# Squares of eight tiles summed on the vector engine and counted once, or counted tile by tile on the tensor engine behind twelve spare transposes

## The chip, the cores and the metric

One core of a Trainium2 chip runs the whole kernel. The metric is device microseconds (us) of one execution. The kernel before took a median of 2697.3 us over three runs (2695.89 to 2697.41).

## What is computed

Two layers of a transformer-like network run over 512 latent tokens and 256 context tokens, with 1024 features each. Only the very first step matters here: the RMS norm of the latents ahead of the first feed-forward block, and the modulation (shift and scale, a product of two conditioning vectors with a weight matrix) that is applied to it.

```
def rms_norm(x, g):
    xf = x.astype(jnp.float32)
    y = xf * lax.rsqrt(jnp.mean(xf * xf, axis=-1, keepdims=True) + EPS)
    return (y * g.astype(jnp.float32)).astype(x.dtype)

def modulate(h, shift, scale):
    return h * (1 + scale) + shift

def half_ffn(h, g, shift, scale, gate, wg, wu, wd):
    return h + 0.5 * gate * swiglu(modulate(rms_norm(h, g), shift, scale), wg, wu, wd)
```

The latents are kept transposed: features on the 128 partitions, tokens along the free dimension. So the 1024 features are eight tiles `xT[0..7]` of 128 x 512 (the context's 256 columns lie beside them), and the mean of the squares of one token is a sum over the partitions of eight tiles.

## The kernel before

The engines are in-order queues: TensorE (PE, with its weight loads PEld), VectorE (DVE), ScalarE (ACT), GpSimd (POOL) and SyncE (SP, which issues almost all transfers). At the kernel's head the instructions stand on PE, DVE and ACT exactly in the order in which the code is written (`chain("te", "ve", "se")` up to the matching `unchain`); every one of them is recorded by one helper, so that nearly all of the profile's rows name its line, L67. Buffers come from rings: `temp()` gives one of five tiles `t`, `slot()` one of 34 tiles `s`, `po()` one of four single PSUM banks, `ps()` one of two double ones. Who takes a buffer waits until its last user is done.

The head goes as follows.

1. The conditioning vectors `sT` land, ACT takes their SiLU, and PE spreads them over all partitions by 16 transposes into two PSUM tiles (`sb_ps`, copied to `sb` much later).
2. The eight tiles `xT[k]` land one after the other. ACT squares each (`stl.square`). The first square goes to a slot `s`, the others to temps `t`; DVE adds squares 1 to 6 to the first (`stl.accumulate`), so that one tile holds the sum of seven.
3. `stl.sums(stl.sq)`: PE clears a bank with a matmul on zeros (`zero`), then counts two tiles into it (`count`): the sum of seven, and the eighth square. To count a tile is four matmuls, one for each 128 tokens, with the squares as weights and a 128 x 2 tile of ones as the moving operand. In float32 each of them is two instructions on PE, each with its weight load, so eight of each kind for a tile.
4. `stl.mean()` and `rsqrt` are nine short DVE instructions on a 128 x 4 tile. Meanwhile PE does five of the eight matmuls of the first modulation group, `wm0_mm(0, 0, 5)` (ten instructions, `ps<-s,sT`). Then `stl.spread(rl)`: four transposes spread the root over the partitions, ACT copies them to `Rs`, PE does the other three matmuls, `wm0_mm(0, 5, KD)`, and ACT copies their result (`sm<-ps`, `wm0_copy(0)`).
5. A loop over eight groups `g` follows: PE computes shift and scale of feature tile `g`, DVE and ACT split modulation weights and scale `xT[g]`, PE begins the first feed-forward products. From about 60 us on the feed-forward block proper runs.

Of the kernel before, what the change touches and what calls it, by code (L numbers as in the profile page):

```python
# [11 lines left out]
AF = mybir.ActivationFunctionType  # L12
# [3 lines left out]
P = 128  # L16
D = 1024
KD = D // P
# [14 lines left out]
LAT = slice(0, SEQ)  # L33
# [15 lines left out]
def tile_net(ctx: ExitStack, tc: tile.TileContext, a, out):  # L49
# [34 lines left out]
    te, ve, se, pe = Engine(nc.tensor, "te"), Engine(nc.vector, "ve"), Engine(nc.scalar, "se"), nc.gpsimd  # L84
# [7 lines left out]
    def nm(s):  # L92
        uid[0] += 1
        return f"{s}{uid[0]}"
# [4 lines left out]
    def temp(dt=F32, w=T):  # L99
        return pool.tile([P, w], dt, name=nm("t"), tag="t", bufs=NTMP)  # L100
# [4 lines left out]
    def ps():  # L105
        return psum.tile([P, 1024], F32, name=nm("ps"), tag="ps", bufs=2)

    def po():
        return psum.tile([P, 512], F32, name=nm("po"), tag="po", bufs=4)

    def f32(t):
        return t.bitcast(F32)
# [7 lines left out]
    ident = const.tile([P, P], F32, name="ident")  # L120
# [15 lines left out]
    xT = [const.tile([P, T], F32, name=f"xT{k}") for k in range(KD)]  # L136
# [105 lines left out]
    def tv(t, s):  # L242

        v = t[:, 0:T].rearrange("p (a b) -> p a b", b=HALF)
        if s == LAT:
            return v[:, :, 0:SEQ // 2]
        if s == CTXS:
            return v[:, :, SEQ // 2:HALF]
        return t[:, 0:SEQ // 2] if s.start == 0 else t[:, HALF:HALF + SEQ // 2]

    def cv(t, s, at=0):

        v = t[:, at:at + s.stop - s.start]
        return v.rearrange("p (a b) -> p a b", a=2) if s in (LAT, CTXS) else v
# [1750 lines left out]
    stl, stc = Stats(LAT, D), Stats(CTXS, D, ps)  # L2005
# [13 lines left out]
    def wm0_high(g):  # L2019
        if g in NATIVE:  # L2020
            return
        parts[g] = [(slot(F32R), slot(F32R)) for _ in range(3)]
        for i, t in enumerate(raws[g]):
            w = 256 * min(3, KD - 3 * i)
            se.copy(parts[g][i][0][:, :w], t[:, :w])
# [45 lines left out]
    for i in range(2):  # L2071
        sb.append(const.tile([P, D], F32, name=f"sb{i}"))
        sb_ps.append(ps())
        for k in range(KD):
            te.transpose(out=sb_ps[i][:, k * P:(k + 1) * P], in_=sT[:, k, i:i + 1].to_broadcast([P, P]), identity=ident)
    for k in range(KD):
        nc.sync.dma_start(out=tv(xT[k], LAT), in_=a["xT"][k, :, LAT].rearrange("p (a b) -> p a b", a=2))
        if k == 0:
            ve.tensor_copy(s4[:, :, 0:2], sT)
            ve.tensor_sub(s4[:, :, 2:4], sT, f32(s4)[:, :, 0:2])  # L2080
            ve.tensor_copy(sel[:, 0:2], ident[0:4, 0:2])
            ve.tensor_add(sel, sel, ident[0:4, 2:4])
        stl.square(tv(xT[k], LAT))
        if k < KD - 1:
            stl.accumulate()
    for i in range(2):
        se.copy(sb[i], sb_ps[i])
    gn.append(cload("gn0", a["gn"][0], [P, 3, KD]))
# [5 lines left out]
    m01 = [const.tile([P, KD, 2], F32, name=f"m01_{j}") for j in range(2)]  # L2094
    for j in range(2):
        mod[(0, j)] = [m01[j][:, :, i] for i in range(2)]
    stl.sums(stl.sq)
    wm0_high(0)
    wm0_low(0, 0)
    stl.mean()  # L2100
# [173 lines left out]
```

## Time and profile before

| | |
|---|---|
| median of three runs | 2697.3 us |
| the profiled execution's own time | 2700.62 us |
| its span, first to last instruction | 2698.8 us |
| PE busy | 2645.2 us, 98% of the span |
| DVE busy | 2047.8 us, 76% |
| ACT busy | 1140.2 us, 42% |
| PE clock granted, mean of the span | 0.996 |

A row of the timeline gives the start (us from the span's start), the time from the first start to the last end of the merged instructions, the engine, the line, the operation, what it writes and reads, the number of merged instructions and, in brackets, how long the engine had been idle before and what ended that. A row of the table by stretches gives, for each stretch, its length, the busy time and number of instructions of PE, PEld, DVE, ACT and POOL, the share of full speed at which the PE clock was granted, the busy share of the transfer engines and the rate in GB/s. The clock is 1.00 where the profile has no record of a cut, which includes the time ahead of its first record.

### The profile page before, as it was taken

Reading aid. Unit: us, or ns where it says so; the run is one execution under the profiler, and the core shown is the slowest. Engines: PE = TensorE matmul, PEld = TensorE weight load, DVE = VectorE, ACT = ScalarE, POOL = GpSimd, SP = SyncE. Lnnn points to the kernel's source line nnn. Section 1 sums busy time; section 2 is a strip of 40 time slices with the busy share of each in tenths; the row PEclk is TensorE's granted clock in tenths of the full one; section 3 lists DMA queues with packets and bytes.
Section 4 is the critical chain, followed back from the end, with each engine's and each line's share of the span. In section 5 each row is a group of like instructions: output and inputs, shape, how many; then the busy total and the mean of one; then the engine's idle time right before and its main releaser. Section 6 shows DMA issues by size and latency. Waiting matters only on the chain. (4 is left out here: it accounts for less than half of the span.)

```text
span 2698.8 us, 40531 instructions
## 1 busy us (share of the span) xinstructions
PE 2645.2 (98%) x16076; PEld 2512.7 (93%) x16076; DVE 2047.8 (76%) x3483; ACT 1140.2 (42%) x1977; POOL 147.5 (5%) x224
## 2 busy tenths in 40 slices
PE   8999999999989999999999999999999999999999
PEld 5999999999888889999999999999998888889988
DVE  6957777777689987777777777777766798776655
ACT  5323333441488633333334433333343488444433
POOL 0000000001230100000000000000000221011110
PEclk9999999999999999999999999999999999999999
DMA  7312333233100321233333223333224101245543
GB/s 254 125 47 94 110 109 110 94 101 136 33 1 9 112 101 56 102 108 110 103 109 105 68 83 104 110 106 105 97 83 162 49 9 40 95 132 169 160 126 118
DMA packets 102606, 266.07 MB, mean 99 GB/s; under 512 B 11920, under 2 KB 40336, under 8 KB 102416
## 3 DMA queue, kind: packets, MB, share of 16 engines
q1 hardware_dynamic: 95792, 249.32, 27.5%
q0 software_dynamic: 6624, 14.16, 2.6%
q8 instruction: 126, 2.06, 0.3%
q14 instruction: 64, 0.52, 0.1%
HBM read 256.63 MB, written 2.10 MB: 96 GB/s over the span
## 5 line engine op out<-in xcount | busy, mean ns | idle before, releaser
L67 PE MATMUL ps<-s,wh 128*128 128x384 f32 (+2 forms) x4224 | 968.4, 338 | 6.2 <-DVE xT L67 2.0
L67 PE MATMUL po<-s,wh 128*128 128x384 f32 (+2 forms) x3216 | 777.7, 327 | 1.1 <-ACT t L67 0.5
L67 PEld LDWEIGHTS ps<-s,wh 128*128 128x128 f32 x4224 | 730.2, 188 | 49.1 <-issue 5.1
L67 PE MATMUL ps<-s,wl 128*128 128x384 f32 (+2 forms) x2112 | 602.3, 337 | 1.3 <-DVE wl L67 1.2
L67 PEld LDWEIGHTS po<-s,wh 128*128 128x128 f32 x3216 | 563.4, 189 | 13.3 <-ACT s L67 0.8
L67 PE MATMUL po<-s,wl 128*128 128x384 f32 (+2 forms) x1608 | 525.6, 327 | 0.0
L67 PEld LDWEIGHTS ps<-s,wl 128*128 128x128 f32 x2112 | 381.2, 188 | 20.1 <-DVE wl L67 3.5
L67 PEld LDWEIGHTS po<-s,wl 128*128 128x128 f32 x1608 | 303.4, 189 | 5.9 <-DVE wl L67 0.2
L67 DVE SCALAR_TENSOR_TENSOR junk<-mr,sb 128x1024 fp8e4<-128x1024 f32 x224 | 273.0, 1219 | 15.0 <-DMA mr<-in_wm_dram 14.2
L67 DVE SCALAR_TENSOR_TENSOR xT<-ps,mod,xT 128x256 f32<-128x256 f32 (+1 forms) x360 | 198.1, 593 | 103.7 <-PE ps L67 101.8
L67 DVE TENSOR_TENSOR wl<-wr,wh 128x1024 fp32r<-128x1024 f32 (+3 forms) x158 | 188.9, 1198 | 110.0 <-ACT wh L67 109.6
L67 ACT CAST wh<-wr 128x1024 fp32r<-128x1024 f32 (+3 forms) x158 | 160.3, 1018 | 153.4 <-PE ps L67 85.9
L67 ACT COPY t<-po 128x384 f32<-128x384 f32 (+2 forms) x218 | 98.4, 451 | 264.1 <-PE po L67 263.5
L67 PE MATMUL po<-s,s 128*128 128x256 f32 (+3 forms) x1216 | 191.7, 309 | 5.5 <-DVE pl L67 2.1
L67 PEld LDWEIGHTS po<-s,s 128*128 128x128 f32 x1216 | 173.8, 191 | 12.6 <-DVE pl L67 2.4
L67 ACT ACTIVATE t<-t 128x384 f32<-128x384 f32 (+1 forms) x144 | 72.0, 500 | 260.6 <-DVE t L67 260.6
L67 DVE TENSOR_TENSOR t<-po,t 128x384 f32<-128x384 f32 (+2 forms) x226 | 117.2, 523 | 35.3 <-ACT t L67 24.9
L67 ACT CAST wh<-ws 128x1024 fp32r<-128x1024 f32 x72 | 75.7, 1052 | 155.1 <-PE ps L67 99.4
L67 ACT CAST s<-t 128x768 fp32r<-128x768 f32 (+3 forms) x144 | 93.0, 650 | 113.4 <-DVE t L67 109.2
L67 DVE TENSOR_TENSOR s<-t,s 128x768 fp32r<-128x768 f32 (+3 forms) x144 | 104.1, 725 | 42.3 <-ACT s L67 41.7
L67 PE MATMUL po<-s,w 128*128 128x384 f32 x648 | 121.0, 334 | 0.0
L67 ACT CAST wh<-t 128x768 fp32r<-128x768 f32 x80 | 66.6, 837 | 115.4 <-PE ps L67 109.0
(197 smaller groups left out, 3321.5 us busy)
## 6 DMA issues: line engine op xcount, KB each, us to landing
mr<-in_wm_dram SPq DMA_DIRECT2D x128, 512.0 KB, 3.2
wr<-in_wg_dram SPq DMA_DIRECT2D x82, 512.0 KB, 3.3
wu<-in_wu_dram SPq DMA_DIRECT2D x72, 512.0 KB, 3.3
t<-in_wd_dram SPq DMA_DIRECT2D x80, 384.0 KB, 3.6
wr<-in_wiT_dram SPq DMA_DIRECT2D x22, 512.0 KB, 3.6
wr<-in_wd_dram SPq DMA_DIRECT2D x20, 512.0 KB, 3.6
ws<-in_wu_dram POOLq DMA_DIRECT2D x36, 256.0 KB, 4.1
wr<-in_wu_dram SPq DMA_DIRECT2D x16, 512.0 KB, 3.3
```

What stands on the lines that cost most here:

```text
L67: f(*args, **kw)
```

## The change

The bank is cleared directly behind the 16 first transposes, and twelve transposes of the identity matrix follow into another bank that nothing reads (`idle`). Each tile's square then goes to a temp, and PE counts it by itself; the additions on DVE and the later call of `sums` are gone.

```
+    stl.zero()
+    idle = po()
+    for _ in range(12):
+        te.transpose(out=idle[:, 0:P], in_=ident, identity=ident)
     for k in range(KD):
         nc.sync.dma_start(out=tv(xT[k], LAT), in_=a["xT"][k, :, LAT].rearrange("p (a b) -> p a b", a=2))
...
-        stl.square(tv(xT[k], LAT))
-        if k < KD - 1:
-            stl.accumulate()
+        sq = temp()
+        se.activation(out=cv(sq, LAT), in_=tv(xT[k], LAT), func=AF.Square)
+        stl.count(sq, k == KD - 1)
...
-    stl.sums(stl.sq)
     wm0_high(0)
```

On PE at the very start of the program, before (`ps1`, `ps2` are the two tiles of `sb_ps`, `po21` the bank of the sums, `s3` the sum of seven squares, `t10` the eighth):

```order
L67 MATMUL ps1_88<-ident_64,sT_82 128x128 x8
L67 MATMUL ps2_98<-ident_64,sT_82 128x128 x8
L67 MATMUL po21_169<-zeros_71,ident_64 128x8
L67 MATMUL po21_169<-ones_69,s3_112 128x2 x4
L67 MATMUL po21_169<-ones_69,t10_139 128x2 x4
L67 MATMUL ps25_191<-s12_149,sT_82 2x256 x3
L67 MATMUL ps25_191<-s13_150,sT_82 2x256 x2
L67 MATMUL po26_197<-ident_64,m23_181 128x128 x4
```

The same place in the changed program (`po3` is the bank of the sums, `po4` the spare one, `t5` to `t12` the eight squares):

```order
L67 MATMUL po3_107<-zeros_71,ident_64 128x8
L67 MATMUL po4_109<-ident_64 128x128 x12
L67 MATMUL po3_107<-ones_69,t5_127 128x2 x4
L67 MATMUL po3_107<-ones_69,t6_134 128x2 x4
L67 MATMUL po3_107<-ones_69,t7_141 128x2 x4
L67 MATMUL po3_107<-ones_69,t8_148 128x2 x4
L67 MATMUL po3_107<-ones_69,t9_155 128x2 x4
L67 MATMUL po3_107<-ones_69,t10_162 128x2 x4
L67 MATMUL po3_107<-ones_69,t11_169 128x2 x4
L67 MATMUL po3_107<-ones_69,t12_176 128x2 x4
L67 MATMUL ps26_222<-s14_190,sT_82 2x256 x3
L67 MATMUL ps26_222<-s15_191,sT_82 2x256 x2
```

Between the clearing and the first modulation matmuls there were two counted tiles; now there are the twelve transposes and eight counted tiles. What follows stands in the same order as before, on every engine.

On ACT, the last four squares before, with what each waits for (a transfer's queue, or another engine's progress):

```order
L67 ACTIVATE t7_127<-xT4_77 128x512 [waits DMAHW5_49]
L67 ACTIVATE t8_131<-xT5_78 128x512 [waits DMAHW6_49]
L67 ACTIVATE t9_135<-xT6_79 128x512 [waits DMAHW7_49,DVE_49]
L67 ACTIVATE t10_139<-xT7_80 128x512 [waits DMAHW0_49,DVE_49]
L67 COPY sb0_87<-ps1_88 128x1024 [waits PE_49]
```

The same rows in the changed program:

```order
L67 ACTIVATE t9_155<-xT4_77 128x512 [waits DMAHW5_49]
L67 ACTIVATE t10_162<-xT5_78 128x512 [waits DMAHW6_49,PE_49,Activation_49]
L67 ACTIVATE t11_169<-xT6_79 128x512 [waits DMAHW7_49,PE_49,Activation_49]
L67 ACTIVATE t12_176<-xT7_80 128x512 [waits DMAHW0_49,PE_49,Activation_49]
L67 COPY sb0_87<-ps1_88 128x1024
```

All eight squares now pass through the ring of five temps, so the sixth, seventh and eighth wait until PE has counted the first, second and third.

## The prediction

> **What bounds the kernel now.** I read the page first, then the timeline of the head, then the same stretch in steps of the granted clock.
>
> ```profile
> span 2698.8 us, 40531 instructions
> 60.00:100.00 40.00, 40.00 (x253) 38.34 (x252) 32.42 (x63) 13.03 (x20) 0.00 (x0) 1.00 0.37 125
> 37.00:41.00 4.00, 4.00 (x28) 2.84 (x26) 4.00 (x9) 2.59 (x6) 0.00 (x0) 1.00 0.85 295
> ```
>
> From 60 us on PE is full (40.00 of 40.00 us). Before that the loop over eight groups is full on DVE and PE (4.00 of 4.00). So a shift of the head's end is passed on whole, unless a transfer is late. The head:
>
> ```profile
> 2.88 3.56 PE L67 MATMUL ps<-ident,sT 128*128 128x128 f32 x16 [2.88 <-ACT sT L67]
> 6.27 0.29 PE L67 MATMUL po<-zeros,ident 128*128 128x8 f32 x2
> 4.21 0.63 ACT L67 ACTIVATE s<-xT 128x512 f32<-128x512 f32 x1 [1.47 <-DMA xT<-in_xT_dram]
> 8.65 1.38 ACT L67 ACTIVATE t<-xT 128x512 f32<-128x512 f32 x2 [0.64 <-DMA xT<-in_xT_dram]
> 9.31 2.29 DVE L67 TENSOR_TENSOR s<-s,t 128x512 f32<-128x512 f32 x3 [0.51 <-ACT t L67]
> 11.05 0.63 ACT L67 ACTIVATE t<-xT 128x512 f32<-128x512 f32 x1 [0.20 <-DMA xT<-in_xT_dram]
> 11.65 1.87 PE L67 MATMUL po<-ones,s 128*128 128x2 f32 x8 [5.10 <-DVE s L67]
> 13.38 1.85 PE L67 MATMUL po<-ones,t 128*128 128x2 f32 x8
> 15.16 4.43 PE L67 MATMUL ps<-s,sT 128*2 128x256 f32 x10
> 15.27 0.16 DVE L67 TENSOR_SCALAR m<-po 128x4 f32<-128x4 f32 x1 [3.58 <-PE po L67]
> 16.85 0.16 DVE L67 SCALAR_TENSOR_TENSOR m<-m,m 128x4 f32<-128x4 f32 x1
> 19.52 0.80 PE L67 MATMUL po<-ident,m 128*128 128x128 f32 x4
> 20.25 1.46 PE L67 MATMUL ps<-s,sT 128*2 128x256 f32 x6
> 20.36 0.59 ACT L67 COPY Rs<-po 128x512 f32<-128x512 f32 x1 [6.86 <-PE po L67]
> 21.74 0.36 ACT L67 COPY sm<-ps 2x256 f32<-2x256 f32 x1 [0.80 <-PE ps L67]
> 22.87 2.43 DVE L67 TENSOR_TENSOR s<-s,s 128x768 fp32r<-128x768 f32 x3 [5.86 <-ACT s L67]
> ```
>
> Squares end at 4.84 to 11.68, some 0.98 us apart, as transfers land. PE idles 5.10 us until the sum of seven is there, counts two tiles, does ten modulation matmuls; the root is ready at 17.0 and waits for PE until 19.52. The last six matmuls end at 21.7, and ACT, then DVE (5.86 us idle) start from there. So the head hangs on PE from 11.65 to 21.7. That is the stretch that the change works on, and there PE ran at two speeds:
>
> ```profile
> 6.22:9.63 3.41, 0.34 (x4) 0.24 (x2) 1.97 (x4) 2.11 (x4) 0.00 (x0) 1.00 1.05 345
> 9.63:13.04 3.41, 1.39 (x7) 1.39 (x7) 1.84 (x4) 3.02 (x5) 0.00 (x0) 0.50 1.03 354
> 13.04:16.45 3.41, 3.41 (x15) 2.50 (x15) 0.98 (x6) 0.46 (x1) 0.00 (x0) 0.50 1.00 373
> 16.45:19.87 3.42, 3.42 (x10) 1.06 (x9) 0.49 (x3) 0.00 (x0) 0.00 (x0) 0.50 1.04 379
> 19.87:23.28 3.41, 2.71 (x15) 1.23 (x13) 0.41 (x1) 2.12 (x4) 0.00 (x0) 1.00 1.03 409
> 571.27 1.03 PE L67 MATMUL ps<-ones,t 128*128 128x2 f32 x8
> 713.79 1.47 PE L67 MATMUL po<-ident,s 128*128 128x128 f32 x12
> 27.87 3.61 PE L67 MATMUL ps<-s,sT 128*2 128x256 f32 x16
> L67 PE MATMUL ps<-ones,t x96: 165/251/272, 571.3 to 2341.4; 128*128 128x2 f32 x96
> L67 PE MATMUL po<-ident,s 128*128 128x128 f32 x42 | 5.6, 273 | 0.0
> L67 PE MATMUL ps<-s,sT x32: 377/379/631, 15.2 to 31.1; 128*2 128x256 f32 x32
> ```
>
> The last number but two of a stretch is the clock. It changes only on a grid of 3.41 us: cut to half at 9.63 behind a stretch with 0.34 us of PE work, given back at 19.87 behind a stretch full of matmuls. Two readings matter. First, the prices: a counted tile costs 13.38 - 11.65 = 1.73 us at half clock, and at full clock 0.89 (1.03 less the last instruction's own 0.25, the middle one of 165/251/272 ns, over seven steps, times eight). A transpose costs (6.27 - 2.88)/16 = 0.212 at half, so the first 16 ran at half though the column has no record yet; at full about 0.11 ((1.47 - 0.27)/11). A modulation matmul costs 0.43 (4.43/10) at half and 0.215 ((3.61 - 0.38)/15) at full. Second, what counts as work for the clock: the stretch 13.04 to 16.45 was busy throughout, 2.2 us of it with counting, and the clock stayed cut; the next, all modulation matmuls, released it. So counting seems not to count.
>
> **The change, part by part.**
>
> Removed: six additions on DVE, 0.69 us each. DVE then idled 3.58 us, so they cost nothing but the last one's place between the seventh square and the first count; in the new order PE waits for squares alone. Count of the seven-sum: removed, and seven tiles put in its place, +6 tiles on PE. At 1.73 that is +10.4 us of PE work, at 0.89 +5.3; of PE's idle 5.10 us from 6.55 to 11.65, the twelve transposes take 1.3 (full clock) to 2.6 (half).
>
> Clearing the bank: moved, same price; it was already done at 6.27. The spare bank is taken at a time when all four are free; the ring then hands each later bank out one place on, and the first product that meets a transposed-into bank comes after 34 us. Cost nothing.
>
> ACT: the sixth, seventh and eighth square wait for counts one to three. The sixth lands at 9.4; count one ends by 8.7 at full clock or 10.7 at half, when PE is behind the squares anyway. Behind them on ACT stand the copies to `sb` and `Rs`; ACT idles 6.86 us ahead of the latter, so that a wait of 2 us is covered. No transfer moves on SP or POOL; one weight load drops a wait.
>
> Now PE's chain in time. PE is past the clearing at 6.45. On the profile's own grid:
>
> - Clock held at 9.63, cut at 13.04 (case A). Transposes to 7.75; six tiles at 0.89 to 13.1; two at 1.73 to 16.5. A stretch of counting ends at 16.45, so no release there; ten modulation matmuls, eight at 0.43 to 19.87, release, two at 0.215 to 20.3; four transposes at 0.11 with 0.15 of waiting, 20.9; six matmuls to 22.2. By the same prices the kernel before comes to 21.4. Difference +0.8.
> - Clock cut at 9.63 (case B). 2.1 tiles by then, 5.9 at 1.73 to 19.8; matmuls at 0.43 until the first full stretch ends at 23.28 (8.1 of ten), then 0.4 and 0.5 to 24.2, six matmuls to 25.5. Difference +4.1.
>
> Which? What the stretch up to 9.63 must hold is bounded by two stretches elsewhere in which counting and other matmuls mix:
>
> ```profile
> 562.59:566.00 3.41, 3.41 (x32) 3.41 (x31) 1.45 (x6) 1.78 (x4) 0.00 (x0) 1.00 0.00 0
> 562.59:566.00 3.41, 2.04 (x16) 2.04 (x16) 0.00 (x0) 1.00 0.00 0
> 719.60:723.01 3.41, 2.70 (x22) 2.53 (x21) 3.14 (x12) 1.84 (x3) 0.00 (x0) 1.00 0.00 0
> 719.60:723.01 3.41, 1.44 (x12) 1.56 (x12) 0.00 (x0) 1.00 0.00 0
> 723.01:733.25 10.24, 8.62 (x35) 8.07 (x35) 3.13 (x5) 3.07 (x6) 0.00 (x0) 0.50 0.01 2
> 712.77:716.19 3.42, 2.50 (x22) 2.21 (x20) 1.88 (x3) 2.85 (x5) 0.00 (x0) 1.00 0.19 74
> 712.77:716.19 3.42, 2.13 (x18) 2.01 (x18) 0.00 (x0) 0.00 (x0) 1.00 0.19 74
> ```
>
> Of each pair the second row is the counting alone (the last pair: the transposes alone). The first stretch has 3.41 - 2.04 = 1.37 us of other work and kept the clock; the second has 2.70 - 1.44 = 1.26 and lost it (the row of 723.01). The third kept it with 2.13 us of transposes and 0.37 of anything else, so transposes hold the clock. The new stretch up to 9.63 has 1.3 us of transposes and some 0.1 left of the first 16: 1.4 to 1.45, by a hair on the side that holds. The next one has counting alone and loses it.
>
> [...]
>
> That is for one position of the grid. Nothing in the program sets where its edges fall, and one profile shows one position; so I weigh all positions alike. Take edges 1.2 us later (7.4, 10.8, 14.2 ...): released at 7.4, half of the transposes are done by then, the stretch to 10.8 holds 0.8 us of them, 1.26 or less, so cut at 10.8; counts end at 19.65, modulation matmuls run at half to 23.9, the end is 26.1 against 22.1 for the kernel before: +4.0. Walking the edges through 3.41 us with these prices gives +0.8 for about a quarter, +4.0 for two fifths, +5.6 for the rest.
>
> [...]
>
> Downstream the shift is passed on: ACT idles for a transfer of the groups' weights first at 40.81, and those loads stand in SP's queue behind others that wait for a buffer (33.27) that the work itself frees, so they shift too:
>
> ```profile
> 33.27 0.33 SPq L196 DMA_DIRECT2D wr<-in_wg_dram  x1
> 40.81 1.81 ACT L67 CAST s<-s 128x768 fp32r<-128x768 f32 x2 [0.46 <-DMA s<-in_wm_dram]
> ```
>
> Sum: case B, +4.1 of PE's chain, 0 for the rest. The profiled execution took 2700.62 (1.8 us beside its span); the median of the three runs shown is 2697.3, 0.12% less, and I add the difference to that median: 2701.4.
>
> **The rivals.**
>
> A, the clock holds through the transposes: +0.8, 2698.1. For it, 1.4 against 1.37; against it, the margin, and the quarter of positions.
>
> C, counting holds the clock as well: counts end at 14.85, the root is ready at 16.9, ten matmuls at 0.215 end at 17.0, the head ends at 18.9: -2.5, 2694.8. Against it the stretch from 13.04 to 16.45 and that of 719.60.
>
> D, slower beyond doubt: the edge falls so that before is released one stretch earlier and after is not. With edges at 8.23, 11.65, 15.06, 18.47, 21.9, 25.3, before gets its full stretch from 15.06 and ends at 20.8; after is cut at 11.65, counts to 19.65, finds its first full stretch only from 21.9, and ends at 26.4: +5.6, 2702.9. What decides is whether an edge lies within about 0.6 us of 15.16, where before's modulation matmuls start.
>
> **How the numbers follow.** About 0.2% (5.4 us) is what a measurement of this kernel can tell from no change. Chances: B 0.42, D 0.22, A 0.26, C 0.08, all else 0.02. B's 2701.4 is the likeliest; 2696.8 to 2703.6 takes in A with a run's scatter of 1.5 and D with 0.7, and leaves out C and the tails. A 10 us cut elsewhere (723.01) may come or go with the grid in either kernel and is in these widths. D lies at the bound, so most of it counts as slower: 0.20. Faster needs twice C's gain: 0.02. Same 0.78.
>
> **What would show it.** Right: PE's eight counted tiles in one run to 19.6 or so, clock 0.50 over most of 10 to 24, first `sm<-ps` copy at 25.4 to 26.5 where it was 21.74, DVE's first split 4 us later, and all later stages alike. A: that copy at 22.5, clock cut at 13. Wrong: counted tiles at 0.9 to the end and the copy before 20 (C); a copy late, but the group loop's end unmoved (a transfer was the bound); or squares on ACT that wait for PE and hold up `Rs`.

## The result, and the profile after

The changed kernel took a median of 2726.46 us (2725.32 to 2728.19, four runs): 1.0107 times the kernel before, with an interval of 1.0092 to 1.0123. That is 29 us more, where 4.1 were forecast and 2703.6 was the upper end of the range.

The page of the changed kernel, its span, its busy times and its clock:

```profile
span 2724.8 us, 40640 instructions
PE 2675.5 (98%) x16136; PEld 2535.8 (93%) x16136; DVE 2044.1 (75%) x3477; ACT 1140.6 (42%) x1977; POOL 147.5 (5%) x224
PEclk8999999999999999999999999999999999999999
```

PE was busy for 30.3 us more (2645.2 before). The 60 added instructions of the head explain some 10 us of that (11.06 + 2.23 us for counting and transposes, where 1.87 + 1.85 us of counting stood). So most of it must lie elsewhere. First the head, in the timeline of PE and ACT:

```profile
2.73 3.65 PE L67 MATMUL ps<-ident,sT 128*128 128x128 f32 x16 [2.73 <-ACT sT L67]
6.45 2.23 PE L67 MATMUL po<-ident 128*128 128x128 f32 x12
8.52 11.06 PE L67 MATMUL po<-ones,t 128*128 128x2 f32 x64
19.51 4.43 PE L67 MATMUL ps<-s,sT 128*2 128x256 f32 x10
23.86 1.11 PE L67 MATMUL po<-ident,m 128*128 128x128 f32 x4
24.91 1.49 PE L67 MATMUL ps<-s,sT 128*2 128x256 f32 x6
26.44 0.36 ACT L67 COPY sm<-ps 2x256 f32<-2x256 f32 x1 [0.84 <-PE ps L67]
27.57 2.43 DVE L67 TENSOR_TENSOR s<-s,s 128x768 fp32r<-128x768 f32 x3 [6.21 <-ACT s L67]
```

The `sm` copy starts at 26.44 where it was 21.74, and DVE's first split at 27.57 where it was 22.87: the head ends 4.7 us later. The table by stretches, cut at the edges of this run's clock grid (the clock is the last number but two; two of the four cut ones are left out):

```profile
4.54:7.96 3.42, 3.42 (x18) 3.42 (x17) 0.00 (x0) 2.22 (x5) 0.00 (x0) 1.00 1.01 315
7.96:11.37 3.41, 3.41 (x34) 3.41 (x32) 0.17 (x1) 1.89 (x4) 0.00 (x0) 1.00 1.08 367
11.37:14.78 3.41, 3.41 (x18) 3.41 (x18) 0.00 (x0) 2.42 (x3) 0.00 (x0) 0.50 1.01 356
18.20:21.61 3.41, 3.41 (x13) 1.90 (x14) 1.47 (x9) 0.00 (x0) 0.00 (x0) 0.50 1.02 397
25.02:28.44 3.42, 2.26 (x11) 0.94 (x9) 0.87 (x1) 2.58 (x5) 0.00 (x0) 1.00 0.91 346
```

The grid's edges lie 1.7 us later than in the profile before (7.96 for 6.22). The clock was released at 7.96, cut at 11.37 behind a stretch of mostly counting, and given back only at 25.02.

Now the rest. If each DVE instruction of one trace is laid beside the same instruction of the other (counted from the end, since the changed kernel has six fewer at the head), the changed kernel is late by this much:

```
time in the kernel before (us)    22.9   60.1  300.2  620.8  740.1  980.6  1540.8  2020.1  end
late by (us)                       4.7    4.7    7.5   11.1    9.6    9.7    16.5    22.5   26.0
```

The delay grows by about 1.2 us in each 100 us of feed-forward work and hardly at all in the attention stretch (740 to 980), where most matmuls have 128 or 256 columns. It falls once, from 13.3 us at 722 to 9.6 at 734: there the kernel before spent 10.24 us at half clock (the prediction's row of 723.01), and the trace of the changed kernel has no such cut. One stretch of 200 us, before and after, in which PE is full in both:

```profile
1100.00:1300.00 200.00, 199.77 (x1150) 198.90 (x1149) 158.55 (x248) 66.71 (x100) 0.00 (x0) 1.00 0.31 105
```

```profile
1100.00:1300.00 200.00, 199.99 (x1135) 199.15 (x1134) 156.07 (x244) 65.44 (x98) 0.00 (x0) 1.00 0.31 106
```

1150 matmuls before, 1135 after (1.3% fewer), at a full clock. By groups of one shape (moving operand, then weights; number of instructions; busy time), before:

```profile
L67 PE MATMUL ps<-s,wh 128*128 128x384 f32 x2640 | 584.3, 335 | 3.2 <-DVE xT L67 1.3 <-DVE s L67 0.8
L67 PE MATMUL po<-s,wh 128*128 128x384 f32 x2160 | 547.8, 334 | 0.0
L67 PE MATMUL po<-s,s 128*128 128x384 f32 x240 | 42.2, 335 | 1.7 <-DVE t L67 1.7
```

and after:

```profile
L67 PE MATMUL ps<-s,wh 128*128 128x384 f32 x2640 | 591.3, 339 | 2.1 <-DVE xT L67 1.3 <-DVE s L67 0.8
L67 PE MATMUL po<-s,wh 128*128 128x384 f32 x2160 | 554.7, 338 | 0.0
L67 PE MATMUL po<-s,s 128*128 128x384 f32 x240 | 42.2, 335 | 1.5 <-DVE t L67 1.5
```

As groups, the 384-column matmuls of a moving operand `s` with weights `wh` got slower by 7.0 and 6.9 us. Those with both operands in the ring `s` kept their 42.2 us. From one start to the next, 23 matmuls of 384 columns at 1210 us stand like this (ns; before, then after):

```
174 173 173 174 173 173 174 173 173 174 173 173 174 173 173 174 173 173 174 173 173 174 173
173 174 175 182 176 173 174 175 182 176 173 174 175 182 176 173 174 175 182 176 173 174 175
```

Every five lose 13 ns: 880 for 867. What the change did to them is said in no line of its diff. SBUF is the memory that holds all buffers here but the PSUM banks; the addresses are those in the built programs, in bytes of a partition. A ring of buffers gets its place in SBUF when the first buffer of it is taken. The first square no longer takes a slot `s` but a temp `t`, so `t` and the small tiles now come first and `s` behind them. The first slot went from byte 54080 to 69824, by 15744 = 30 x 512 + 384 (five temps of 3072 bytes and 384 bytes of small tiles), while the weights `wh`, `wl` stayed at 189248 and up. So `wh` began 135168 = 264 x 512 bytes behind the first slot in the kernel before, and begins 119424 = 233 x 512 + 128 behind it in the changed one. Slots are 3072 bytes long and weight buffers 4096, both multiples of 512, so every pair is off by the same 128 (the expectations below count the other way round and say 384).

### The profile page after: what moved, and what is told of

It is laid out like the page before. It is cut to its first block, busy times and chain, and to the rows that moved or that the text cites. A ratio compares the mean times of both kernels' runs of the same rounds, so it can differ in the third digit from the quotient of the medians.

```text
span 2724.8 us, 40640 instructions
## 1 busy us (share of the span) xinstructions
PE 2675.5 (98%) x16136; PEld 2535.8 (93%) x16136; DVE 2044.1 (75%) x3477; ACT 1140.6 (42%) x1977; POOL 147.5 (5%) x224
```

## The experiments

Four theories stood: the distance of the operands in SBUF, the chip, the 120 more PE instructions (60 matmuls and their 60 weight loads) or the shifted ring of PSUM banks, and the absolute place of `s`.

**e1: the changed kernel, with the old addresses.**

```
-        sq = temp()
+        sq = temp() if k else slot()
```

> The changed kernel with one edit: the first square goes to a slot s again, so that the ring s is again the first that is taken and the rings s, t and m get their old addresses in SBUF (first slot at byte 54080 of a partition in place of 69824). Counting on TensorE and the twelve transposes stay. Theory 1, the place of the moving operands (s) against the weights (wh, wl at 189248 and on) slows TensorE by 1.5% in the dense stretches: the time falls to about 2702 us, that is 2697.4 plus the 4.7 us by which the head ended later; the step of a 384-column matmul is 173.3 ns throughout. Theory 2, the chip or its state made the difference and not the program: the time stands to the kernel before as before. Theory 3, the 120 more TensorE instructions or the shifted ring of PSUM banks: it stays at about 2726 us, with 176 ns.

Measured: 2702.81 us beside 2698.89 for the kernel before on the same chip, ratio 1.0017 (1.0008 to 1.0027), so 4.6 us more by the ratio and 3.9 by the medians. The `sm` copy stood at 26.47, as in the changed kernel, and 200 us held this:

```profile
1100.00:1300.00 200.00, 199.77 (x1151) 198.90 (x1150) 157.20 (x245) 66.59 (x101) 0.00 (x0) 1.00 0.33 104
```

1151 matmuls where the kernel before had 1150. One changed line takes the larger part of the loss away, and the counting, the transposes, the added instructions and the shifted banks are all still there. What is left is the head's delay. The rivals chip, instructions and banks fall.

**e2: the kernel before, with the new addresses.**

```
+    temp(), small(KD)
     nc.sync.dma_start(out=sT, in_=a["cT"])
```

> The kernel before, with one temp t and one small tile m taken (and not used) ahead of everything, so that the rings t, m and s get the addresses of the changed kernel. No instruction is added or moved. Theory 1 (place of s against the weights): 2697.4 + 21.3 = about 2719 us, with a head that ends at 21.7 us as before, and steps of 173 to 182 ns, mean 176, for 384-column matmuls. Theory 2 (chip) and theory 3 (instructions, PSUM banks): 2697 us, no difference.

Measured: 2721.16 us, ratio 1.0087 (1.0070 to 1.0105). Its group by shape:

```profile
L67 PE MATMUL ps<-s,wh 128*128 128x384 f32 x2640 | 591.1, 339 | 2.5 <-DVE xT L67 1.3 <-DVE s L67 0.8 <-ACT s L67 0.4
L67 PE MATMUL po<-s,s 128*128 128x384 f32 x240 | 42.2, 335 | 1.6 <-DVE t L67 1.6
```

591.1 us as in the changed kernel, though its instructions are those of the kernel before. Two buffers that nobody uses cost 0.9%.

**e3, e4, e6, e7, e10: which distance, and of what.** All are the kernel before with an unused tile of n bytes at one place. In e3, e6 and e7 it stands between `s`, `t`, `m` and all later rings (n = 128, 64, 256), in e4 ahead of everything (128), in e10 between the raw weights `wr` and the split weights `wh` (128):

```
 e3, e6, e7:
+    pool.tile([P, n // 4], F32, name="pad", tag="pad", bufs=1)
     for tag in ("st", "st2"):
 e4:
+    const.tile([P, 32], F32, name="pad")
     ones = const.tile([P, 2], F32, name="ones")
 e10:
         raw = wload(a[("wg", "wu")[j % 2]][0, j // 2], 1024)
+        if j == 0:
+            pool.tile([P, 32], F32, name="pad", tag="pad", bufs=1)
```

> The kernel before, with an unused tile of 128 bytes per partition between the rings s, t, m and all rings behind them, so that the weights wh, wl start 128 bytes later (189376) while s stays (54080). Theory 1: what matters is the distance of weights and moving operand modulo some power of two up to 512 bytes; it is a multiple of 512 in the kernel before and 384 beyond one in the changed kernel, and here 384 too; so about 2718 us. If absolute places of s count instead: 2697 us. Theories 2 and 3: 2697 us.

> The kernel before, with an unused tile of 128 bytes per partition ahead of everything but the first constants, so that s and the weights both start 128 bytes later (54208 and 189376). Theory 1 (distance): 2697 us, no difference. If the absolute place of either counts: up to 2718 us.

> The kernel before, with the rings behind s, t and m moved by 64 bytes (weights at 189312). The distance from the weights to the moving operand is then 64 bytes short of a multiple of 512. If any distance but a multiple of 256 or 512 slows TensorE: 2719 to 2722 us, 173.3 ns grows to about 176. If only an odd multiple of 128 does: 2699 us.

> The kernel before, with the rings behind s, t and m moved by 256 bytes (weights at 189504). If the distance counts modulo 256: no difference, 2699 us, 173.3 ns. If modulo 512: 2720 us, 176 ns.

> The kernel before, with 128 unused bytes between the raw weights wr and the split weights wh, wl, so that wr, Rs, ot and wu stay where they were and only what TensorE loads as weights (and the rings behind, mr among them) moves. Theory 1 (distance between TensorE's two operands): 2720 to 2722 us, 176 ns. If the distance of s to wr, Rs or ot, which VectorE and ScalarE use, made the loss: 2699 us, 173.3 ns.

| | s starts at | wh starts at | ratio to before | interval |
|---|---|---|---|---|
| e3 | 54080 | 189248 + 128 | 1.0094 | 1.0074 to 1.0115 |
| e4 | 54080 + 128 | 189248 + 128 | 1.0003 | 0.9990 to 1.0015 |
| e6 | 54080 | 189248 + 64 | 1.0030 | 1.0019 to 1.0042 |
| e7 | 54080 | 189248 + 256 | 0.9997 | 0.9988 to 1.0006 |
| e10 | 54080 | 189248 + 128, `wr` unmoved | 1.0070 | 1.0055 to 1.0085 |

The same group of 384-column matmuls, in e3, then in e6:

```profile
L67 PE MATMUL ps<-s,wh 128*128 128x384 f32 x2640 | 590.7, 339 | 2.2 <-DVE xT L67 1.3 <-DVE s L67 0.8
```

```profile
L67 PE MATMUL ps<-s,wh 128*128 128x384 f32 x2640 | 587.7, 337 | 4.8 <-ACT s L67 1.9 <-DVE xT L67 1.4 <-DVE s L67 0.8
```

Moving both by 128 (e4) costs nothing, so it is not the absolute place that counts. Moving the weights and all rings behind `s` by 128 costs as much as in the changed kernel, by 256 nothing, by 64 a third. For e6 I had expected all or nothing; it was neither. Raw weights and the tiles of DVE and ACT in between may stay where they are (e10); that one was nearer to 0.7% than to the 0.8 of the forecast, within its interval.

How much a matmul loses depends on its number of columns as well. The same operands with 512 and with 256 columns, in the kernel before, in the changed kernel and in e6:

```profile
L67 PE MATMUL ps<-s,wh 128*128 128x512 f32 x832 | 273.6, 393 | 2.6 <-ACT wh L67 1.8 <-ACT s L67 0.5 <-DVE xT L67 0.3
L67 PE MATMUL ps<-s,wh 128*128 128x256 f32 x752 | 163.5, 284 | 0.5 <-DVE xT L67 0.4
```

```profile
L67 PE MATMUL ps<-s,wh 128*128 128x512 f32 x832 | 276.6, 396 | 2.1 <-ACT wh L67 1.2 <-ACT s L67 0.7 <-DVE xT L67 0.2
L67 PE MATMUL ps<-s,wh 128*128 128x256 f32 x752 | 163.5, 284 | 0.5 <-DVE xT L67 0.3
```

```profile
L67 PE MATMUL ps<-s,wh 128*128 128x512 f32 x832 | 277.7, 398 | 0.7 <-ACT s L67 0.4 <-DVE xT L67 0.2
L67 PE MATMUL ps<-s,wh 128*128 128x256 f32 x752 | 161.0, 282 | 0.3
```

From start to start, 512 columns take 227 ns on average in the first, 233 in the other two; 256 columns take 120, 119 and 116. So the third that e6 loses is a balance: its 512-column matmuls lose as much as at 128 bytes off, its 384-column ones little, and its 256-column ones gain.

**e9: the changed kernel, with the same 128 bytes.** The edit is that of e3, on the changed kernel.

> The changed kernel as it is, with s at 69824, and an unused tile of 128 bytes between s, t, m and the rings behind them, so that the weights go from 189248 to 189376. The same 128 bytes that cost the kernel before 0.9%. The distance of weights and moving operand becomes a multiple of 256 again. Theory 1 (distance modulo 256): 2702 to 2704 us, 0.1 to 0.2% over the kernel before, 173.3 ns a step. If the place of s itself or the order of the rings counts: 2720 to 2726 us, 176 ns.

Measured: 2702.68 us beside 2699.01, ratio 1.0017 (1.0004 to 1.0029). The padding that cost the kernel before 0.9% gives the changed one as much back, with `s` at its new place and the rings in their new order; the weights then begin 119552 = 467 x 256 bytes behind the first slot. Its head also showed the case that the prediction called A:

```profile
6.17 1.51 PE L67 MATMUL po<-ident 128*128 128x128 f32 x12
7.52 8.94 PE L67 MATMUL po<-ones,t 128*128 128x2 f32 x64
9.59:13.00 3.41, 3.41 (x31) 3.41 (x31) 0.17 (x1) 2.93 (x4) 0.00 (x0) 0.95 0.99 358
13.00:16.41 3.41, 3.41 (x18) 3.39 (x18) 0.00 (x0) 0.00 (x0) 0.00 (x0) 0.50 1.04 399
```

On this run's grid the clock was held until 12.7 (0.95 of the stretch to 13.00); 64 counting instructions took 8.94 us in place of 11.06, and the `sm` copy came at 22.24.

**e5: counting without the twelve transposes** (on e1).

```
-    idle = po()
-    for _ in range(12):
-        te.transpose(out=idle[:, 0:P], in_=ident, identity=ident)
```

> The changed kernel with the old addresses (first square in a slot) and without the twelve spare transposes and their bank: counting tile by tile alone. Theory 1, the clock: counting does not hold it, so it is half for most of the counting with the transposes or without them; the first sm copy on ACT at 24 to 27 us as with them (26.5), the time within 1.5 us of that kernel's, 2701 to 2704 us, 0.1 to 0.25% over the kernel before. Theory 2, the twelve transposes hold the clock through the counting: without them the copy comes 3 us later or more, 2705 us or over. Theory 3, the transposes are the cost (1.3 to 2.6 us ahead of the counting): the copy near 23.9, 2700 us.

Measured: 2702.42 us, ratio 1.0009 (1.0001 to 1.0018) beside 1.0017 with them (1.0008 to 1.0027); the copy at 27.23. The two intervals overlap: over 12 and 10 runs, the transposes bring nothing that these runs can tell. Theory 3, that they are the cost, asked for a copy near 23.9 and is not borne out by this one trace, in which the clock was never released ahead of 25.7 (56 counting instructions in 12.09 us, ten modulation matmuls in 4.43, four transposes in 1.10 from 24.70). How much of the 0.1 to 0.2% is theirs stays open.

**e8: VectorE's sums as before, and the idle time filled** (on the kernel before).

```
+    idle = po()
+    for _ in range(44):
+        te.transpose(out=idle[:, 0:P], in_=ident, identity=ident)
     for k in range(KD):
         nc.sync.dma_start(out=tv(xT[k], LAT), in_=a["xT"][k, :, LAT].rearrange("p (a b) -> p a b", a=2))
```

> The kernel before, sums on VectorE as before, with 44 transposes of the identity into a spare bank between the first 16 transposes and the clearing, so that TensorE is busy until about 11 to 12 us. Theory 1, the clock: the clock is released by 9.6 and is still full when the two tiles are counted and for the modulation matmuls, so these take half of their time: first sm copy at 17.6 to 18.5 us in place of 21.7, time lower by 3.5 us: 2695 us beside a before of 2699, ratio 0.9987. Theory 2, the head's end does not matter for the end of the kernel (a transfer is the bound): the copy comes early, the time is the same.

Measured: 2695.93 us beside 2698.77, ratio 0.9991 (0.9982 to 1.0000). The timeline and the stretches:

```profile
6.16 5.15 PE L67 MATMUL po<-ident 128*128 128x128 f32 x44
11.29 1.03 PE L67 MATMUL po<-ones,s 128*128 128x2 f32 x8
12.18 1.03 PE L67 MATMUL po<-ones,t 128*128 128x2 f32 x8
13.14 2.32 PE L67 MATMUL ps<-s,sT 128*2 128x256 f32 x10
17.47 0.36 ACT L67 COPY sm<-ps 2x256 f32<-2x256 f32 x1 [0.80 <-PE ps L67]
6.52:9.93 3.41, 3.41 (x33) 3.41 (x32) 2.79 (x5) 2.49 (x5) 0.00 (x0) 1.00 1.10 350
9.93:13.35 3.42, 3.42 (x32) 3.28 (x31) 0.87 (x3) 2.49 (x4) 0.00 (x0) 1.00 1.00 363
16.76:20.17 3.41, 2.12 (x14) 1.11 (x12) 1.58 (x2) 2.35 (x4) 0.00 (x0) 1.00 1.03 405
20.17:27.00 6.83, 6.33 (x24) 2.79 (x22) 5.40 (x12) 4.82 (x8) 0.00 (x0) 0.50 1.04 400
```

Counting a tile costs 1.03 in place of 1.87 us, ten modulation matmuls 2.32 in place of 4.43, and the copy comes 4.3 us earlier. That is theory 1's account of the head. Of the 4.3 us, DVE was still 2.8 ahead at 40 us: the clock was cut once more at 20.17, behind a stretch in which PE was busy for 2.12 of 3.41 us. The ratio is the lowest here, but its interval ends at no difference, so a gain in time is likely and not shown.

## Why the prediction was wrong

The step that failed is a line that priced a move at nothing. The prediction said of the buffers that the ring "hands each later bank out one place on" and "Cost nothing", summed "case B, +4.1 of PE's chain, 0 for the rest", and gave 0.02 to "all else". It followed the rings for who waits for whom, and the banks of PSUM, but it never asked where in SBUF a ring stands. That 0 measured +0.87% (e2) and took 0.90% away when undone (1.0107 to 1.0017, changed kernel to e1): some 21 to 24 of the 29 us (26.0 less 4.7 in the two traces; 0.90% of 2697). The prediction's own sign "all later stages alike" is the one that failed. The profile of before could not show this price, since slots and split weights stand at a multiple of 512 bytes from each other in all of it; the place could have been seen before the run, from the change of the first tile taken out of each ring.

The steps on the head held. Its end came 4.7 us late in the profile; by ratio, e1 lost 0.17% or 4.6 us, where case B said +4.1 and its neighbour D +5.6. The two profiles lie on different grids, so that 4.7 came so near to 4.1 is in part luck. The run's grid (edges at 7.96, 11.37, ... 25.02) was near the example worked out for D: cut at 11.65 there and 11.37 here, counting to 19.65 there and 19.51 here, release at 25.3 and 25.02, head's end at 26.4 (the last matmul) there, the copy at 26.44 here. Case A was seen as well (e9). Case C was not: in the traces with counting tile by tile the clock was cut during the counting (at 11.37 in the changed kernel, at 12.7 in e9) or not yet released (e5), and e1's copy came as late as the changed kernel's (26.47 and 26.44).

That the transposes hold the clock, read from one stretch before, was shown: in e8 the stretch 6.52 to 9.93 holds transposes alone (33 in 3.41 us), and the clock stays at 1.00 in the next, where a counted tile took 1.03 us.

That the delay of the head is passed on was right for e1: its trace is 4.73 us later than that of before at 22.9 and at 50 us, and 5.1 later at 620. Behind that other differences mix in: it is 7.3 late at 722 (why was not traced), 3.5 at 734, past the cut of the clock at 723 that only the trace of before has and that the prediction allowed for, and 3.3 at the end.

## What to carry to other kernels

Before a change to buffers is priced at nothing, compare the addresses, not only the waits: taking one ring's first buffer ahead of another's can move thousands of operands. This kernel, half of whose matmuls have 384 columns, was fastest with TensorE's two operands a multiple of 256 bytes apart in SBUF (ratios 0.9997 and 1.0003 in e7 and e4, beside 1.0030 at 64 bytes off and 1.0070 to 1.0094 at 128), and 128 bytes of unused padding decided 0.9% of its time. And where the clock falls behind idle time (here at 9.63 us in the kernel before, after a stretch with 0.34 us of PE work in 3.41) or behind counting with 2-column matmuls (at 11.37 in the changed kernel, after a stretch with 2.85 us of it), plain spare work until the real work comes did more for the head (e8, the copy 4.3 us earlier) than handing it the small instructions early (4.7 us later), though over the whole kernel e8's gain stays at the edge of what was measured.

## What the runs showed of the hardware that was not expected

- A matmul of 384 columns steps at 173.3 ns with moving operand and weights a multiple of 256 bytes apart (kernel before), at 176 on average 128 bytes off (173, 174, 175, 182, 176 in turn in the changed kernel), and at 174 at 64 bytes off (e6; group of 2640: 584.3 us in the kernel before, 590.7 in e3, 587.7 in e6). With 512 columns it is 227, 233 and 233 ns (group of 832 in the kernel before, the changed kernel and e6: 273.6, 276.6 and 277.7 us), and with 256 columns 120, 119 and 116 (group of 752: 163.5, 163.5 and 161.0 us): there the multiple of 256 is the slowest of the three. So 128 bytes cost 1.5% of a step of 384 columns. Why is not settled: no run tried a cause by itself, and no distances but 64, 128 and 256 were tried.
- The clock's grid of 3.41 us lay elsewhere in each of four executions: the first recorded cut came at 9.63, 11.37, 12.7 and 20.17 us (kernel before, changed kernel, e9, e8), and no two of these are a multiple of 3.41 us apart. Later cuts came and went: the one at 723 us (0.50 from 723.01 to 733.25 in the kernel before), worth 3.7 us between the two traces (13.3 late at 722, 9.6 at 734), is not in the trace of the changed kernel, whose clock is 1.00 from 25.02 to the end, nor in e1, whose delay falls from 7.3 to 3.5 us there, nor in e2 or e8, whose profiled runs had a mean clock of 0.999 (10.24 us at half would take off 0.0019).
